# Hybrid attention layer on one core: pre-norm gain of token tiles 4 to 7 multiplied in by POOL, and a written-out order for all engines

## The chip, the core and the metric

One core of one Trainium2 chip. The core has a TensorE (PE), which multiplies matrices and transposes, a VectorE (DVE), a ScalarE (ACT), a GpSimd (POOL), and a SyncE (SP), whose queue here issues the DMA transfers. The metric is the time of one execution in microseconds (us) on the device, as the median of three runs.

## What is computed

One layer of an encoder for 1024 tokens of width 1024, all in float32. The reference, cut to what matters:

```python
h = rms_norm(x, norm_pre_g)                       # y * rsqrt(mean(y*y) + eps) * g
sb_q, sb_k, sb_v, sb_g, c_q, c_kv, k_rope, mla_g = split(h @ w_in)
sb_o  = stick_breaking_attention(sb_q, sb_k, sb_v)            # 8 heads of 64, strictly causal
sb_y  = head_rms_norm(sb_o, sb_out_norm_g) * silu(sb_g)
q     = rms_norm(c_q, q_norm_g) @ w_uq                        # 8 heads: 64 plain + 32 rotary
k_nope, v = split(rms_norm(c_kv, kv_norm_g) @ w_ukv)
mla_o = latent_attention(q_nope, rope(q_rope), k_nope, rope(k_rope), v)   # chunk-causal softmax
mla_y = head_rms_norm(mla_o, mla_out_norm_g) * silu(mla_g)
x = x + rms_norm(concat(sb_y, mla_y) @ w_out, norm_post_g)
x = x + rms_norm(p @ w_ple, ple_norm_g) * sigmoid(x @ w_ple_gate + b_ple_gate)
```

## The kernel before

**Precision and tiling.** Tokens go in eight tiles of 128. A float32 matrix product is made of three products of a faster type (float32r): each operand is split into a high half (a rounded copy) and a low half (the value less that copy), and high x high, high x low and low x high are added in PSUM. So most results go through the helper `split` (line 848): one copy, mostly on ACT, and one subtraction on DVE or POOL. The transposed, normalized input is kept as `hh` and `hl` (high and low halves, two buffers of four token tiles each). In the names of the trace, `h` is such a buffer, `u` and `f` are SBUF buffers of two pools (28 and 10 buffers of 4 KB per partition), `a` and `t` are PSUM banks of two pools (3 and 5), `ident` is the identity matrix for transposes.

**Stages.** First the value projection of the tiles (`xv_gen`, line 996, up to about 75 us), then the other projections, woven between 16 pairs of attention units (to about 625 us); `e1` (output projection and post-norm), `e2a` and `e2b` (gate product, made with seven instead of eight block products, and the final sum) end it. The per-layer embedding (`ple_gen`, line 1249) is one of the woven pieces; it transposes `p_in`, splits it into `pt`, and multiplies it by `w_ple`.

**The pre-norm (lines 889 to 931).** `x_norm(t)` squares a tile on ACT, makes the reciprocal root on POOL (`rstd_pow`, tile `sr`), and multiplies the tile by it on DVE. The gain `norm_pre_g` varies along the row, and can be put in at two places. With `t < GAINS` (line 69, 8: all tiles) it is put in behind the transposes, where it is one number per partition (`g_pre`): `x_tr(t)` makes, for each of eight blocks of 128x128, an ACT copy with that scale into `hh` and a DVE operation (`scalar_tensor_tensor`) into `hl`. Otherwise it is put in ahead of the transposes, along the row: by DVE in one step with `t < EARLY` (line 58), or else by POOL in a step of its own; `x_tr` then uses `split`, once for each half of the tile. `gain()` (line 905) spreads the gain over the partitions for these two cases; with `GAINS = 8` it isn't called.

**The order.** The body doesn't issue instructions; it records them (`Recorder.add`, line 414), 6,621 in all, 3,905 of them on PE. A list of numbers, `FLIP` (line 239), moves two-input operations between DVE and POOL, and copies between ACT and DVE. Each has a priority: its place in the recording, plus 336 in a piece marked low, plus a shift of its piece from the table `SHIFT` (line 76). `schedule` (line 533) then plays the program through with costs of its own: of the instructions of an engine that are ready, the one with the lowest priority number goes first. Buffers of a pool are handed out in the order of `turn`, also shifted by piece. `issue` (line 722) issues all in the order found; line 754 is the one line at which every instruction of the body stands in the trace. The engine queues run in that order, and the semaphores make each instruction wait for its inputs and its buffer.

**Other pieces the text speaks of.** `close` (in `e2b`, line 1669) makes an output piece: a DVE addition that reads PSUM, a sigmoid on ACT, a multiplication, an addition, and the store. The last block product of the program is made in two halves of 256 columns.

Of the kernel before, what the change touches and what calls it, by code (L numbers as in the profile page):

```python
# [1846 lines left out]
```

## Time and profile before

| | us |
|---|---|
| median of three runs | 765.4 |
| the three runs | 765.14, 765.4, 769.76 |
| the profiled execution, its own time | 765.5 |
| its span, from the first to the last instruction of the trace | 763.7 |

One execution is profiled; everything read from the trace belongs to it, and its time lies 0.1 us above the median. Its own time is 1.8 us more than its span. A busy time is the sum of what the trace gives for an engine's instructions. The ends of matmuls are modelled, so that successive ones overlap: two rows of PE can begin closer together than the first one lasts. Where the timeline puts a run of like instructions on one row, the row has the start of the first and the time to the end of the last.

### The profile page before, as it was taken

What the parts mean: (1) busy time and instruction counts of PE and PEld (TensorE: products, weight loads), DVE (VectorE), ACT (ScalarE), POOL (GpSimd) and SP (SyncE); (2) the same over time, 40 slices, a digit from 0 to 9 for tenths busy, and PEclk for the clock granted to TensorE, in tenths of its full rate; (3) what the DMA queues carried; (4) which work ended last, traced back from release to release, by engine and by line L of the source; (5) the groups of instructions that cost most, each with busy time, mean ns of one, the idle gap of its engine ahead of it and who ended that gap; (6) DMA issues with size and microseconds to landing.
All of it is one profiled execution on the core that took longest, in us unless ns stands there. A gap on an engine that the chain in (4) does not pass through costs nothing.

```text
span 763.7 us, 11831 instructions
## 1 busy us (share of the span) xinstructions
PE 751.0 (98%) x3905; PEld 621.0 (81%) x3905; DVE 630.6 (83%) x1238; ACT 399.7 (52%) x962; POOL 321.7 (42%) x306
## 2 busy tenths in 40 slices
PE   7999999999999999999999999999999999999997
PEld 4888998878888878888887788888888888888876
DVE  6966355599958869888888999989899998789987
ACT  7633133244534785666657767767765541451221
POOL 2141113104411269869888521430363126464642
PEclk9999999999999999999999999999999999999999
DMA  9753103587998643656545884878436367272332
GB/s 324 247 168 129 74 33 120 190 313 279 341 355 272 214 132 137 198 189 209 175 138 162 270 298 145 286 267 286 144 116 212 125 248 244 87 276 83 110 111 83
DMA packets 101982, 148.71 MB, mean 195 GB/s; under 512 B 7448, under 2 KB 55072, under 8 KB 101920
## 3 DMA queue, kind: packets, MB, share of 16 engines
q1 hardware_dynamic: 101920, 147.95, 57.3%
q8 instruction: 31, 0.51, 0.3%
q14 instruction: 31, 0.25, 0.1%
HBM read 101.26 MB, written 46.66 MB: 194 GB/s over the span
## 4 chain that ended last, share of the span: by engine, by line
PE 88%; ACT 5%; DVE 3%; DMA 2%; issue 1%; POOL 0%; SPq 0%; ACTq 0%; DVEq 0%; POOLq 0%
PE a L754 62%; PE t L754 26%; ACT u L754 3%; DVE u L754 1%; DMA u<-k_d 1%; DMA v_d<-f 1%; ACT L754 1%; ACT h L754 1%; ACT f L754 1%; DVE nm L754 1%; DVE f L754 1%; DMA u<-v_d 0%; SPq L754 0%; DVE t L754 0%; DVE nms L754 0%
## 5 line engine op out<-in xcount | busy, mean ns | idle before, releaser
L754 POOL TENSOR_TENSOR u<-u,u 128x512 f32<-128x512 f32 (+14 forms) x134 | 190.5, 1436 | 140.1 <-ACT u L754 74.8
L754 PE MATMUL a<-h,f 128*128 128x512 f32 x864 | 240.7, 404 | 0.0
L754 PEld LDWEIGHTS a<-h,f 128*128 128x128 f32 x864 | 155.2, 189 | 26.4
L754 DVE TENSOR_TENSOR u<-t,u 128x512 fp32r<-128x512 f32 (+4 forms) x284 | 150.6, 555 | 22.2 <-ACT u L754 12.8
L754 PE MATMUL t<-u,u 128*128 128x512 f32 (+4 forms) x580 | 151.0, 367 | 1.0 <-DMA u<-k_d 0.5
L754 PE MATMUL a<-u,u 128*128 128x512 f32 (+2 forms) x522 | 133.4, 370 | 0.1
L754 PE MATMUL t<-ident,u 128*128 128x128 f32 (+1 forms) x793 | 126.4, 273 | 1.4 <-DVE nms L754 0.5
L754 ACT CAST u<-t 128x512 fp32r<-128x512 f32 (+3 forms) x192 | 87.4, 490 | 75.4 <-PE t L754 49.0
L754 PEld LDWEIGHTS t<-u,u 128*128 128x128 f32 x580 | 103.0, 189 | 20.2 <-ACT u L754 3.2
L754 PE MATMUL a<-h,u 128*128 128x512 f32 (+1 forms) x492 | 117.3, 391 | 0.1
L754 ACT ACTIVATE u<-t 128x512 f32<-128x512 f32 (+5 forms) x208 | 92.0, 515 | 47.2 <-PE t L754 38.6
L754 PEld LDWEIGHTS t<-ident,u 128*128 128x128 f32 (+1 forms) x793 | 97.1, 140 | 22.3 <-DVE u L754 2.9
L754 PEld LDWEIGHTS a<-h,u 128*128 128x128 f32 x492 | 89.6, 188 | 20.3 <-DVE u L754 0.5
L754 PEld LDWEIGHTS a<-u,u 128*128 128x128 f32 x522 | 91.7, 188 | 16.9 <-DVE u L754 2.0
L754 DVE TENSOR_TENSOR u<-u,u 128x512 fp32r<-128x512 f32 (+8 forms) x88 | 79.6, 917 | 5.3 <-ACT u L754 3.5
L754 ACT ACTIVATE u<-t,nms 128x384 f32<-128x384 f32 (+5 forms) x96 | 55.2, 581 | 39.7 <-DVE nms L754 39.4
L754 DVE TENSOR_TENSOR_SCAN u<-u 128x320 f32<-128x320 f32 (+4 forms) x64 | 64.6, 1011 | 13.6 <-ACT u L754 12.4
L754 ACT ACTIVATE f<-a 128x512 bf16<-128x512 f32 (+2 forms) x64 | 34.2, 539 | 51.5 <-PE a L754 48.4
L754 POOL MEMSET u<- 128x128 f32 x64 | 13.0, 216 | 102.1 <-PE a L754 56.4
L754 DVE TENSOR_TENSOR u<-a,u 64x512 f32<-64x512 f32 (+4 forms) x75 | 47.8, 647 | 8.2 <-ACT u L754 6.9
L754 DVE TENSOR_REDUCE nm<-t 128x1 f32<-128x384 f32 (+5 forms) x96 | 51.8, 547 | 1.9 <-PE t L754 1.2
L754 PE MATMUL a<-u,h 128*128 128x512 f32 x192 | 47.0, 399 | 1.5 <-ACT h L754 1.4
(111 smaller groups left out, 801.1 us busy)
## 6 DMA issues: line engine op xcount, KB each, us to landing
u<-q_d SPq DMA_DIRECT2D x64, 256.0 KB, 4.4
u<-k_d SPq DMA_DIRECT2D x16, 512.0 KB, 5.1
u<-v_d SPq DMA_DIRECT2D x16, 512.0 KB, 5.4
u<-in_w_ple_gate_dram SPq DMA_DIRECT2D x16, 512.0 KB, 6.7
f<-in_w_in_dram SPq DMA_DIRECT2D x14, 512.0 KB, 5.1
v_d<-u SPq DMA_DIRECT2D x12, 512.0 KB, 3.1
f<-in_x_dram SPq DMA_DIRECT2D x9, 512.0 KB, 4.4
q_d<-u SPq DMA_DIRECT2D x9, 512.0 KB, 4.4
```

What stands on the lines that cost most here:

```text
L754: x["fn"](*[place(a) for a in x["args"]], **{k: place(a) for k, a in x["kw"].items()})
```

## The change

The gain of tiles 4 to 7 is put in ahead of the transposes, along the row, by POOL; tiles 0 to 3 stay as they were. `gain()` spreads the gain by one DMA. The order of every engine is now a table: `BASE` gives the priority of each of the 6,578 instructions, and `schedule` takes each engine's instructions strictly in that order instead of choosing among those that are ready; `TURNS` gives the turn of each tile for its buffer; `FLIP` is a new list, and `SHIFT` is empty. [...] The diff, with the tables cut to a line:

```diff
-EARLY = 7
+EARLY = 0
-GAINS = 8
+GAINS = 4
-SHIFT = {
-    0: (1204, 1209), 1: (-381, -413), 2: (-586, -394), 3: (-857, -953), 4: (-1159, -1106), 5: (-11, -91),
...
+SHIFT = {}
 FLIP = (
...
+BASE = (
+    17, 19, 15, 21, 16, 22, 18, 24, 2, 3, 4, 5, 6, 7, 8, 9, 10, 11, 12, 13, 31, 32, 35, 57, 26, 40, 39, 76, 53, 70,
...
+TURNS = (
+    28, 37, 33, 36, 2, 225, 298, 292, 287, 297, 306, 235, 308, 296, 304, 300, 317, 316, 310, 160, 283, 69, 58, 60,
...
@@ in Recorder.tile
-            self.tiles[key].update(turn=self.turn(1), turn0=len(self.ins), chunk=self.chunk)
+            self.tagged += 1
+            place = TURNS[self.tagged - 1] if TURNS else len(self.ins)
+            self.tiles[key].update(turn=place + SHIFT.get(self.chunk, (0, 0))[1], turn0=place, chunk=self.chunk)
@@ Recorder.turn
-    def turn(self, by=0):
-        return len(self.ins) + SHIFT.get(self.chunk, (0, 0))[by]
+    def turn(self):
+        i = len(self.ins)
+        return (BASE[i] if BASE else i + (LOW if self.low else 0) + self.bias) + SHIFT.get(self.chunk, (0, 0))[0]
@@ in schedule
+        line = {e: sorted((i for i in range(n) if ins[i]["eng"] == e), key=lambda i: (-ins[i]["prio"], -i))
+                for e in engines}
...
-                if avail[e]:
+                if BASE:
+                    if not line[e] or need[line[e][-1]]:
+                        continue
+                    s = max(free[e], ready[line[e][-1]])
+                elif avail[e]:
...
+            if BASE:
+                i = line[e].pop()
@@ gain
-                gb["pre"], row = k4(dt=F32, name="gb_pre"), k4(dt=F32, name="gb_row")
-            SP.dma_start(row[0:1], norm_pre_g[0:1, :])
-            for v in half:
-                ps = ps_t()
-                mm(ps, ones, row[0:1, v], start=True, stop=True)
-                ACT.copy(gb["pre"][:, v], ps)
+                gb["pre"] = k4(dt=F32, name="gb_pre")
+            bcast(gb["pre"], norm_pre_g, D)
```

The diff also adds four switches (`EVACS`, `NORMS`, `HALVES`, `SPREAD`) for other ways to make some steps. All are zero, and with zeros the steps are as before; `BYDVE` is now called `MASKER`.

What the new order looks like is shown at three places. The first is PE at the first tile of the per-layer embedding, whose `p_in` is `f_3760` before. Before:

```order
L754 MATMUL a_127<-u_3957,u_3534 128x384 x2
L754 MATMUL a_127<-u_3961,u_3534 128x256 x2
L754 MATMUL t_179<-ident,u_3796 128x128
L754 MATMUL t_179<-ident,u_3854 128x128
L754 MATMUL t_179<-ident,u_3937 128x128
L754 MATMUL a_127<-u_3767,u_3534 128x256 x2
L754 MATMUL t_172<-ident,f_3760 128x128
L754 MATMUL t_224<-ident,f_3760 128x128 x2
L754 MATMUL a_308<-f_3634,f_4051 128x512
L754 MATMUL a_308<-f_3658,f_4051 128x512
```

After; `f_3551` is now that `p_in`:

```order
L1074 MATMUL a_217<-u_3928,u_3710 128x384
L1074 MATMUL t_196<-ident,f_3551 128x128
L1074 MATMUL a_217<-u_3928,u_3710 128x384
L1074 MATMUL a_217<-u_3933,u_3710 128x256
L1074 MATMUL a_217<-u_823,u_3710 128x256
L1074 MATMUL a_217<-u_3760,u_3710 128x256
L1074 MATMUL a_217<-u_823,u_3710 128x256
L1074 MATMUL t_189<-ident,u_3763 128x128
L1074 MATMUL t_189<-ident,u_3826 128x128
L1074 MATMUL t_242<-ident,f_3551 128x128
L1074 MATMUL t_189<-ident,u_3904 128x128
L1074 MATMUL t_242<-ident,f_3551 128x128
```

Each tile of `p_in` needs two transposes into one bank (`t_172` before, `t_196` after; the first of the two stands further ahead), then its split copies, and then the matmuls that read them (`a_308` before, `a_251` after). Before, only two transposes of the next tile stand between the last transpose into `t_172` and the first matmul of `a_308`. After, five matmuls and five transposes stand between the last transpose into `t_196` and the first matmul of `a_251`, which is the row after these.

The second place is POOL at the start, where `sr` is the reciprocal root of a token tile's norm. Before:

```order
L754 TENSOR_TENSOR sr_168<-sm_166,nhalf 128x1
L754 TENSOR_TENSOR sr_199<-sm_194,nhalf 128x1
L754 TENSOR_TENSOR sr_270<-sm_266,nhalf 128x1
L754 TENSOR_TENSOR u_506<-f_361,u_506 128x512
L754 TENSOR_TENSOR sr_287<-sm_284,nhalf 128x1
L754 TENSOR_TENSOR u_533<-f_371,u_500 128x512
L754 TENSOR_TENSOR u_549<-f_365,u_549 128x128
L754 TENSOR_TENSOR f_568<-f_467,f_528 128x832
```

After; `u_321` is the gain, spread over all partitions, and `u_185`, `u_187` and `f_301` are token tiles:

```order
L1074 TENSOR_TENSOR sr_205<-sm_201,nhalf 128x1
L1074 TENSOR_TENSOR sr_280<-sm_274,nhalf 128x1
L1074 TENSOR_TENSOR u_185<-u_185,u_321 128x1024
L1074 TENSOR_TENSOR u_423<-u_255,u_403 128x1024
L1074 TENSOR_TENSOR u_187<-u_187,u_321 128x1024
L1074 TENSOR_TENSOR u_488<-u_327,u_447 128x1024
L1074 TENSOR_TENSOR u_485<-f_412,u_485 128x512
L1074 TENSOR_TENSOR sr_297<-sm_293,nhalf 128x1
L1074 TENSOR_TENSOR f_301<-f_301,u_321 128x1024
```

The multiplications by the gain stand between the last reciprocal roots and the low halves of the first weights. The DMA that spreads the gain is 16th in SP's queue.

The third place is the end, on DVE and on POOL, where the last output piece of 512 columns is closed. Before, on DVE:

```order
L754 TENSOR_TENSOR u_7213<-a_308,u_7213 128x512
L754 TENSOR_TENSOR u_6841<-a_235,u_6841 128x256
L754 TENSOR_TENSOR u_7135<-u_7135,u_7213 128x512
L754 TENSOR_TENSOR u_6841<-a_127,u_6841 128x256
L754 TENSOR_TENSOR u_6504<-u_6504,u_7135 128x512
L754 TENSOR_TENSOR u_6504<-u_6504,u_7135 128x256
L754 TENSOR_TENSOR u_7135<-u_7135,u_6841 128x256
L754 TENSOR_TENSOR u_6504<-u_6504,u_7135 128x256
```

and on POOL:

```order
L754 TENSOR_TENSOR u_7090<-u_7090,u_6826 128x512
L754 TENSOR_TENSOR u_7112<-u_7112,u_7213 128x512
L754 TENSOR_TENSOR u_7285<-u_7169,u_7285 128x512
L754 TENSOR_TENSOR u_6723<-u_6723,u_7112 128x512
L754 TENSOR_TENSOR u_7135<-u_7135,u_6841 128x256
```

After, on DVE:

```order
L1074 TENSOR_TENSOR u_6801<-a_143,u_6801 128x512
L1074 TENSOR_TENSOR u_7165<-u_7165,u_7141 128x512
L1074 TENSOR_TENSOR u_6801<-a_217,u_6801 128x256
L1074 TENSOR_TENSOR u_6735<-u_6735,u_7165 128x512
L1074 TENSOR_TENSOR u_6801<-a_251,u_6801 128x256
L1074 TENSOR_TENSOR u_7165<-u_7165,u_6801 128x256
```

and on POOL:

```order
L1074 TENSOR_TENSOR f_6505<-f_6505,u_7095 128x512
L1074 TENSOR_TENSOR u_7141<-u_7141,u_6699 128x512
L1074 TENSOR_TENSOR u_6902<-u_6902,u_7177 128x512
L1074 TENSOR_TENSOR u_7165<-u_7165,u_6801 128x256
L1074 TENSOR_TENSOR u_6735<-u_6735,u_7165 128x256 x2
```

The output tile is `u_6504` before and `u_6735` after. Before, DVE makes the last two additions of 256 columns; after, both are POOL's, and the last of them stands behind a multiplication that stays on DVE.

## Rows read from the trace of the kernel before

**Rows 1.** The page, its part 1: busy time, share of the span and number of instructions of each engine.

```profile
PE 751.0 (98%) x3905; PEld 621.0 (81%) x3905; DVE 630.6 (83%) x1238; ACT 399.7 (52%) x962; POOL 321.7 (42%) x306
```

**Rows 2.** Groups of PE's matmuls and transposes by shape, over the span: line, engine, operation, out<-in, shape, count | busy us, mean ns of one | idle time before them, and what ended it.

```profile
L754 PE MATMUL a<-h,f 128*128 128x512 f32 x864 | 240.7, 404 | 0.0
L754 PE MATMUL t<-ident,u 128*128 128x128 f32 x792 | 126.3, 273 | 1.4 <-DVE nms L754 0.5 <-DVE u L754 0.4 <-DVE sm L754 0.2
L754 PE MATMUL a<-h,u 128*128 128x512 f32 x468 | 114.5, 397 | 0.1
L754 PE MATMUL a<-u,u 128*128 128x512 f32 x334 | 97.9, 404 | 0.0
L754 PE MATMUL t<-u,u 128*128 128x512 f32 x235 | 67.4, 402 | 0.1
L754 PE MATMUL a<-u,h 128*128 128x512 f32 x192 | 47.0, 399 | 1.5 <-ACT h L754 1.4
L754 PE MATMUL a<-f,h 128*128 128x416 f32 x192 | 39.4, 357 | 0.7 <-DVE f L754 0.7
L754 PE MATMUL t<-u,u 128*128 128x384 f32 x115 | 30.2, 354 | 0.1
L754 PE MATMUL a<-f,f 128*128 128x512 f32 x96 | 29.0, 413 | 0.7 <-DVE f L754 0.3 <-ACT f L754 0.3
L754 PE MATMUL a<-u,u 128*128 128x256 f32 x125 | 24.1, 288 | 0.1
L754 PE MATMUL t<-u,u 128*128 128x448 f32 x80 | 23.2, 380 | 0.0
L754 PE MATMUL a<-u,u 128*128 128x384 f32 x63 | 18.7, 352 | 0.0
L754 PE MATMUL t<-u,u 128*128 128x320 f32 x80 | 17.1, 321 | 0.5 <-DMA u<-k_d 0.5
L754 PE MATMUL t<-u,u 128*128 128x256 f32 x70 | 16.6, 305 | 0.3 <-ACT u L754 0.3
L754 PE MATMUL t<-ident,f 128*128 128x128 f32 x80 | 12.0, 272 | 0.0
...
L754 PE MATMUL a<-still 128*128 128x512 bf16 x12 | 5.2, 627 | 2.2 <-DVE still L754 2.2
```

**Rows 3.** The timeline of PE, at 27, 403 to 408 and 640 us: start, us, engine, line, operation, out<-in, shape, count, and in brackets idle time before it and its releaser.

```profile
27.70 1.91 PE L754 MATMUL t<-ident,u 128*128 128x128 f32 x16
...
403.34 0.27 PE L754 MATMUL t<-ident,f 128*128 128x128 f32 x1
403.37 1.40 PE L754 MATMUL a<-u,u 128*128 128x512 f32 x5
404.61 0.60 PE L754 MATMUL t<-u,u 128*128 128x320 f32 x3
...
407.63 0.49 PE L754 MATMUL t<-ident,f 128*128 128x128 f32 x3
408.42 1.55 PE L754 MATMUL a<-f,f 128*128 128x512 f32 x5 [0.30 <-DVE f L754]
...
639.65 12.88 PE L754 MATMUL a<-h,u 128*128 128x512 f32 x55
```

**Rows 4.** The timeline of all engines at the end of the span, in the same columns.

```profile
750.04 8.56 PE L754 MATMUL a<-h,u 128*128 128x512 f32 x48
...
758.21 0.93 POOL L754 TENSOR_TENSOR u<-u,u 128x256 f32<-128x256 f32 x1 [0.87 <-ACT u L754]
...
758.98 1.84 DVE L754 TENSOR_TENSOR u<-u,u 128x512 f32<-128x512 f32 x4
```

**Rows 5.** The busy time of the engines by stretch: from:to, length, then busy us (and count) of PE, PEld, DVE, ACT and POOL, the granted clock of PE, the busy share of the DMA engines, and GB/s.

```profile
2.20:25.00 22.80, 21.00 (x87) 13.27 (x88) 16.23 (x43) 16.91 (x42) 4.99 (x8) 1.00 1.05 365
25.00:75.00 50.00, 50.00 (x240) 40.94 (x239) 36.91 (x95) 22.00 (x65) 11.52 (x11) 1.00 0.48 162
75.00:250.00 175.00, 174.31 (x883) 147.81 (x882) 121.34 (x275) 66.05 (x181) 38.10 (x52) 1.00 0.63 216
250.00:400.00 150.00, 149.89 (x834) 123.53 (x833) 126.36 (x200) 100.63 (x228) 114.98 (x101) 1.00 0.54 176
400.00:500.00 100.00, 97.52 (x544) 80.83 (x543) 93.18 (x220) 70.35 (x181) 44.15 (x41) 1.00 0.71 237
500.00:625.00 125.00, 124.70 (x707) 105.84 (x707) 115.70 (x241) 80.09 (x190) 33.98 (x37) 1.00 0.58 196
...
550.00:600.00 50.00, 50.00 (x277) 42.23 (x276) 47.09 (x92) 31.22 (x76) 20.20 (x22) 1.00 0.52 163
```

**Rows 6.** Groups by shape of ACT, DVE and POOL, in the columns of rows 2.

```profile
L754 DVE TENSOR_TENSOR u<-t,u 128x512 fp32r<-128x512 f32 x124 | 81.9, 680 | 14.0 <-ACT u L754 7.1 <-PE a L754 3.2 <-DMA k_d<-u 2.8
...
L754 ACT CAST u<-t 128x512 fp32r<-128x512 f32 x97 | 55.0, 599 | 42.7 <-PE t L754 27.2 <-PE a L754 7.5 <-DVE u L754 3.6
...
L754 DVE SCALAR_TENSOR_TENSOR h<-t,g_pre,h 128x128 fp32r<-128x128 f32 x64 | 17.6, 343 | 4.2 <-ACT h L754 4.0
...
L754 ACT ACTIVATE h<-t,g_pre 128x128 fp32r<-128x128 f32 x64 | 17.6, 396 | 2.8 <-PE t L754 1.9 <-DVE h L754 0.8
...
L754 POOL TENSOR_TENSOR f<-f,f 128x1024 fp32r<-128x1024 f32 x4 | 9.6, 2406 | 10.5 <-DVE f L754 10.5
```

**Rows 7.** The group of DVE's two-input operations of 128x512 with both inputs in SBUF, in the same columns.

```profile
L754 DVE TENSOR_TENSOR u<-u,u 128x512 fp32r<-128x512 f32 x32 | 30.1, 948 | 2.0 <-ACT u L754 1.9
```

More of the change, by code (lines that the diff above doesn't have):

```diff
@@ L359, in __init__ @@
         self.chunk = 0
+        self.tagged = 0
         self.thread = ""
@@ L655, in schedule @@
             s, e = best
[L656 to L659 removed]
+            if BASE:
+                i = line[e].pop()
+            else:
+                while pend[e] and pend[e][0][0] <= s:
+                    r, i = heapq.heappop(pend[e])
+                    heapq.heappush(avail[e], (ins[i]["prio"], i))
+                _, i = heapq.heappop(avail[e])
             x = ins[i]
@@ L838, in block_kernel @@
     gate_d = [dram([128, S], f"gate_d{i}") for i in range(8)]
+    rs_d = [dram([8, 128], f"rs_d{i}") for i in range(16)]
     y_d = dram([4, 128, KB, 2, 128], "y_d")
@@ L885, in x_load @@
         xt = k4(dt=F32, name="xt")
-        SP.dma_start(xt, x[0, t * 128:(t + 1) * 128, :])
+        for v in half if t == 0 and HALVES[0] else [slice(0, D)]:
+            SP.dma_start(xt[:, v], x[0, t * 128:(t + 1) * 128, v])
         x_tiles[t] = xt
@@ L891, in x_norm @@
         junk = k2((128, 1024), BF16, "junk")
-        ss, ms, rs = small("ss", 1, 4), small("sm", 1, 4), small("sr", 1, 4)
-        ACT.activation(junk, xt, AF.Square, accum_out=ss)
-        DVE.tensor_scalar(ms, ss, 1.0 / D, EPS, ALU.mult, ALU.add)
+        ss, ms, rs = small("ss", 2, 4), small("sm", 1, 4), small("sr", 1, 4)
+        if t == 0 and HALVES[0]:
+            for i, v in enumerate(half):
+                ACT.activation(junk[:, v], xt[:, v], AF.Square, scale=D ** -0.5, accum_out=ss[:, i:i + 1])
+            DVE.tensor_scalar(ms, ss[:, 0:1], ss[:, 1:2], EPS, ALU.add, ALU.add)
+        else:
+            ACT.activation(junk, xt, AF.Square, accum_out=ss[:, 0:1])
+            DVE.tensor_scalar(ms, ss[:, 0:1], 1.0 / D, EPS, ALU.mult, ALU.add)
         rstd_pow(rs, ms)
@@ L1027, in c_gen @@
         c_tr(NT - 1, last)
-    R.piece("warm") if hasattr(R, "piece") else None
     R.piece("warm")
@@ L1064, in proj, with qk_evac @@
         yield 1.3
-    def qk_evac(dst):
+    def qk_evac(dst, k):
         def evac(ps, n):
             t = k4((128, 2, 512), name="qkhl")
-            split(t[:, 0], t[:, 1], ps, heng=ACT)
+            if EVACS[2 * k + n]:
+                raw = k2(dt=F32, name="qkraw")
+                ACT.copy(t[:, 0], ps)
+                ACT.copy(raw, ps)
+                POOL.tensor_tensor(t[:, 1], raw, f(t[:, 0]), ALU.subtract)
+            else:
+                split(t[:, 0], t[:, 1], ps, heng=ACT)
             SP.dma_start(dst[:, :, half[n]], f(t))
@@ L1241, in half_norm @@
             ACT.activation(junk, ps, AF.Square, accum_out=ss[:, n:n + 1])
-            DVE.tensor_tensor(yg[:, half[n]], ps, gb[:, half[n]], ALU.mult)
+            if on_act:
+                ACT.copy(yg[:, half[n]], ps)
+            else:
+                DVE.tensor_tensor(yg[:, half[n]], ps, gb[:, half[n]], ALU.mult)
             yield 0.0
@@ L1272, in mms @@
                     yield 1.3
-                o, rs = yield from half_norm(mms, gb_ple, "ple_o")
-                DVE.tensor_scalar(o, o, rs, None, ALU.mult)
+                o, rs = yield from half_norm(mms, gb_ple, "ple_o", NORMS[t] == 1)
+                if NORMS[t] == 2:
+                    POOL.tensor_scalar(o, o, rs, None, ALU.mult)
+                elif NORMS[t]:
+                    DVE.scalar_tensor_tensor(o, o, rs, gb_ple, ALU.mult, ALU.mult)
+                else:
+                    DVE.tensor_scalar(o, o, rs, None, ALU.mult)
                 SP.dma_start(ple_d[t * 128:(t + 1) * 128, :], o)
@@ L1338, in sb_rows @@
                 ACT.activation(row[:, ks], ps[:, 0:h], AF.Sigmoid, scale=SB_SCALE)
+            if MASKER[4 * i[0] + 2 * i[1] + s] == 2:
+                for t, fill in ((u, 1.0), (row, 0.0)):
+                    t = t[:, nk - 128:nk]
+                    POOL.affine_select(t, t, pattern=[[-1, 128]], compare_op=ALU.is_gt, fill=fill, base=0,
+                                       channel_multiplier=1)
             ev, od = (slice(j, nk, 2) for j in range(2))
@@ L1451, in finish3 @@
         SP.dma_start(gl, gate_d[c][:, half[s]])
-        rx, ps = k2(dt=F32, name="rx"), ps_t()
-        ACT.copy(rx.rearrange("q (g d) -> q g d", d=64),
-                 bass.AP(tensor=rs.tensor, offset=rs.offset, ap=[rs.ap[0], [1, 8], [0, 64]]))
-        for a in range(4):
-            PE.transpose(ps[:, a * 128:(a + 1) * 128], rx[:, a * 128:(a + 1) * 128], ident)
-        DVE.tensor_tensor(ot, ps, ot, ALU.mult)
+        ps = ps_t()
+        if SPREAD[2 * c + s]:
+            PE.transpose(ps[0:8, 0:128], rs, ident)
+            rt, fac = k2((128, 128), F32, name="rt"), k2(dt=F32, name="fac")
+            ACT.copy(rt[0:8], ps[0:8, 0:128])
+            d = rs_d[2 * c + s]
+            SP.dma_start(d, rt[0:8])
+            for e in range(2):
+                SP.dma_start(fac[64 * e:64 * e + 64].rearrange("q (t n) -> q t n", t=4),
+                             d[4 * e:4 * e + 4].rearrange("(o t) n -> o t n", o=1).broadcast_to([64, 4, 128]))
+            choice(13).tensor_tensor(ot, ot, fac, ALU.mult)
+        else:
+            spread(ps, ot, rs)
         choice(14).tensor_tensor(ot, ot, gl, ALU.mult)
@@ L1464, in finish3, with spread @@
             SP.dma_start(y_d[:, :, c].rearrange("t q a n -> q t a n"), f(y))
+    def spread(ps, ot, rs):
+        rx = k2(dt=F32, name="rx")
+        ACT.copy(rx.rearrange("q (g d) -> q g d", d=64),
+                 bass.AP(tensor=rs.tensor, offset=rs.offset, ap=[rs.ap[0], [1, 8], [0, 64]]))
+        for a in range(4):
+            PE.transpose(ps[:, a * 128:(a + 1) * 128], rx[:, a * 128:(a + 1) * 128], ident)
+        DVE.tensor_tensor(ot, ps, ot, ALU.mult)
     def run_later(force=False):
@@ L1603, in e1 @@
         mms = big(ys, lambda kb, n: wo[0][n][:, kb], lambda kb, n: wo[1][n][:, kb])
-        yg, rs = yield from half_norm(mms, gb["post"], "yg")
+        yg, rs = yield from half_norm(mms, gb["post"], "yg", NORMS[8 + t])
+        if NORMS[8 + t]:
+            POOL.tensor_tensor(yg, yg, gb["post"], ALU.mult)
         DVE.scalar_tensor_tensor(xt, yg, rs, xt, ALU.mult, ALU.add)
@@ L1692, in e2b @@
                     R.piece(f"e{t}")
-                    close(1, 0, product(xs, 4, v), w, w, v, DVE)
+                    ps = product(xs, 4, v)
+                    step = 128 if v.start and HALVES[1] else 256
+                    for a in range(v.start, v.stop, step):
+                        close(1, 0, ps, w, w, slice(a, a + step), DVE)
                 continue
```

39 lines of the change are left out of this document (22 added, 17 removed), and 634 rows, old and new, of tables (BASE, FLIP, SHIFT, TURNS).

## The prediction

> **What bounds the kernel.** I read the page's totals first, then the PE stream in order of time, then its groups by shape, then the stretches, and only then single operations. The totals say that PE is busy 98% of the span [rows 1]. Busy time alone doesn't prove a PE limit, because the ends of matmuls are modelled: in the shape table a 512-column matmul "lasts" 404 ns [rows 2]. So I took the rate from a run without a wait: 55 of them fill 12.88 us, less the last one's 0.40, which is 0.231 us from start to start. Sixteen transposes fill 1.91 us, less the last one's 0.27: 0.109 us each [rows 3].
>
> With these the shape table [rows 2] gives the time that PE needs if nobody makes it wait. 2,189 matmuls of 512 columns x 0.231 = 505.9 us. The narrower ones by columns: 192 of 416 (36.1), 178 of 384 (30.8), 195 of 256 (22.5), 80 of 448 (16.2), 80 of 320 (11.6): 117.2. 872 transposes x 0.109 = 95.2. The twelve idle ones at the start: 5.2. That is 723.5 for 3,798 of 3,905; the other 107 cost 4 to 20 more. PE runs from 2.2 us (its idle time ahead of the first one, [rows 2]) to 758.6 (the last row of 48 starts at 750.04 and fills 8.56, [rows 4]): 756.4. So 12 to 29 us are lost to waits; I take 20. This is all that any order can win, since the change leaves the number and shapes of PE's 3,905 matmuls as they are.
>
> Where is it lost? The stretches [rows 5] show the granted clock at 1.00 throughout, and PE idle 1.8 us up to 25 us (22.8 less 21.0), nothing from 25 to 75, 0.7 up to 250, 0.1 up to 400, 2.5 from 400 to 500, 0.3 up to 625. Visible idle time is the smaller part, and I share the rest out like it: 2.5 of these 5.4 is nearly half of 20, but that stretch also has the longest single waits, which show most; I take 7 us for 400 to 500. DVE is busy 93.2 of 100 us there.
>
> The time sum is made against the profiled execution: 765.5 us, 1.8 more than its span, and 0.1 above the median of the three runs. A measurement of this kernel can tell about 1%, 7.7 us, from no change.
>
> **Part 1: the gain of tiles 4 to 7.** Removed: 32 ACT and 32 DVE operations of 128x128, each 17.6/64 = 0.275 us [rows 6], 8.8 us on either engine. Added: 8 copies of 128x512 (five on ACT at 0.60, three on DVE at 0.68) and 8 subtractions on DVE at 0.68. ACT is relieved by 5.8 us and DVE by 1.4. POOL gets four multiplications of 128x1024; the nearest row is 2.41 us, so 9.6 us. None of this lies on the path of the end: from 25 to 75 us, where these tiles are made ready, PE is busy 50.00 of 50 while POOL works 11.5 and ACT 22.0 [rows 5]. What hides the multiplications is POOL's idle time; if that cover is gone, each is a link ahead of eight transposes, and what then is late is PE (a rival below). Queued behind a multiplication on POOL are the next rstd power and the low halves of weights. Value 0; bounds: -0.5 (an earlier evacuation) and +9.6. The row of the gain, now spread over all partitions, is one more DMA of 0.52 MB in SP's queue, 16th there, behind the x tiles. In the first 25 us the DMAs move 365 GB/s [rows 5], so later transfers can slip by 1.4 us: 0, up to +1.4.
>
> **Part 2: finer interleaving on PE.** In PE's order I count 254 runs of transposes before and 455 after. The price of a cut is read at a lone transpose: from 403.34 to 404.61 stand one transpose and five matmuls [rows 3]; 1.27 less 5 x 0.231 is 0.115, against 0.109 within a run. 201 more runs x 0.006 = +1.2 us; bounds 0 and twice that.
>
> **Part 3: who does what.** Matching the two orders, 62 two-input operations go from DVE to POOL and 69 from POOL to DVE; 91 copies go from DVE to ACT and 74 back. By the time at which they stand in the trace, and with the durations of like shapes, DVE loses 9.0 us of work from 75 to 250, gains 16.7 from 250 to 400 (26 operations come from POOL, 5 go), loses 4.5 from 400 to 500 and 8.2 from 500 to 625. In 400 to 500, where DVE is short, I count its relief in full, 4.5 us, and add 0.46 for one wait that the order itself removes: three transposes at 407.63 need 0.33, and the matmul that reads their copy starts at 408.42, released by DVE [rows 3]. After the change five matmuls stand between the first of these transposes and its matmul. Together -5.0; bounds 0 and -7. Elsewhere, 75 to 250 and 500 to 625, 1.0 us of PE is visibly idle: -0.5, bounds 0 and -1.5. For 250 to 400 I take 0: DVE rises from 126.4 to some 143 of 150 us, 95%, but from 550 to 600 it is at 94% and PE waits for nothing [rows 5]. The bound is +7.5, worked out as a rival.
>
> [...] DVE's subtraction with one input in PSUM takes 0.68 us; with both inputs in SBUF it takes 0.95 on average for the same shape [rows 6, 7]. [...]
>
> **Part 4: the end.** The last multiply-add after PE's last matmul moves in part to POOL: the final addition of 256 columns now runs there. Its nearest row is 0.93 us; DVE's last four take 1.84 together, 0.46 each [rows 4]. So +0.5; bounds 0 and +1.0 (the first half's two operations are now POOL's as well).
>
> **Sum.** 0 + 1.2 - 5.0 - 0.5 + 0 + 0.5 = -3.8: 765.5 - 3.8 = **761.7 us**, half a per cent faster. Its own range is 758 to 766.
>
> **Rivals.** *Most waits go.* The order is made anew for every instruction, and the 13 us that I leave lost outside 400 to 500 are within its reach. All 7 there and half of the 13 gone, plus 1.7 for parts 2 and 4: 765.5 - 13.5 + 1.7 = 753.7. For it: PE's need doesn't grow, and the crowded engine of each stretch is relieved (POOL in 250 to 400, DVE in 400 to 625). Against it: waits are spread thin, a few tenths each.
>
> *DVE becomes the bound from 250 to 400.* Its 26 new operations make it 95% busy over 150 us. From the point where DVE falls behind PE's order, PE loses as it does now from 400 to 500, 7 in 100: 10.5, of which I put 3 down as lost already. With no relief in 400 to 500 either, as its own order is as tight, 765.5 + 7.5 + 1.7 = 774.7, slower. Against it: 550 to 600, and that POOL has fewer operations there to hold DVE up.
>
> [...]
>
> *POOL's gain is late.* PE stands before the transposes of four tiles for 2.4 us each: 761.7 + 9.6 = 771.3. It decides if POOL's multiplication ends after PE reaches that tile. Against it: POOL is idle more than three quarters of that stretch.
>
> **How the numbers follow.** Forecast 0.40 (761.7); most waits go 0.34 (753.7); DVE from 250 to 400 0.13 (774.7); port 0.08 (767.2); late gain 0.05 (771.3). More than 1% faster, below 757.8, is the second alone: 0.34. More than 1% slower, above 773.2, is the third alone: 0.13. Within 1%: 0.40 + 0.08 + 0.05 = 0.53. The range for 8 in 10 reaches from 752, a little below the best case, to 771, which leaves out most of the worst.
>
> **What would show it.** Right: PE starts and ends its 3,905 matmuls with the same two rates; its idle time from 400 to 500 falls from 2.5 us to under 1; DVE's busy time there falls by some 4 us; PE has none from 25 to 75; the span's end lies 5.3 to 6 us behind PE's last matmul instead of 5.1. Wrong in size: PE idle in 250 to 400 above 2 us (then DVE there), or PE's last matmul before 750 (then the waits outside 400 to 500 went too). Wrong in mechanism: idle PE ahead of transposes between 25 and 75 us with POOL as releaser, or transposes that cost more than 0.12 us alone.

## The result, and the profile after

The changed kernel takes 758.5 us (median of four runs, 757.3 to 760.13), 8.1 us less than the kernel before in the same comparison (766.6); the ratio is 0.9891, with an interval of 0.9876 to 0.9906. That is 1.1% faster, at the edge of what can be told, and inside the range given for the forecast (758 to 766), at its lower end. The forecast gain was 3.8 us, so the measured one is more than twice that. The profiled execution took 757.3 us, the fastest of the four; its span is 755.2.

The totals of the page, which answer to [rows 1]:

```profile
PE 744.9 (99%) x3905; PEld 617.3 (82%) x3905; DVE 602.4 (80%) x1207; ACT 399.5 (53%) x948; POOL 319.3 (42%) x303
```

PE has the same 3,905 instructions, and DVE is busy 28 us less. The stretches after, in the columns of [rows 5]:

```profile
2.00:25.00 23.00, 21.79 (x96) 14.87 (x97) 16.84 (x44) 16.88 (x43) 6.10 (x10) 1.00 1.02 357
25.00:75.00 50.00, 50.00 (x241) 41.20 (x240) 28.72 (x65) 19.87 (x46) 20.93 (x15) 1.00 0.51 178
75.00:250.00 175.00, 175.00 (x894) 149.03 (x893) 115.69 (x274) 66.79 (x192) 50.68 (x56) 1.00 0.63 216
250.00:400.00 150.00, 148.68 (x826) 121.57 (x825) 133.23 (x228) 96.77 (x212) 84.72 (x81) 1.00 0.54 175
400.00:500.00 100.00, 100.00 (x576) 84.45 (x575) 94.44 (x226) 74.95 (x191) 46.85 (x46) 1.00 0.77 253
500.00:625.00 125.00, 125.00 (x698) 104.95 (x697) 109.71 (x228) 81.94 (x193) 44.84 (x42) 1.00 0.58 191
```

PE is idle in 250 to 400 us now (1.3), and no longer in 400 to 500 and 75 to 250. But the stretches are of time, and PE is ahead of before by 2 us at 25 and by 8 at 500; so from here on I go by PE's own progress: matmuls and transposes are numbered in PE's order, 0 to 3,904. **Loss** is the time from the start of each matmul to the next, less what its shape takes at full rate, which I read from runs of like ones without a wait in the trace of before (0.2315 us for 512 columns, down to 0.118 for 256; 0.1095 for a transpose), summed over the records; the 0.08 us by which a matmul behind a transpose starts early in the records (one starts 0.03 us behind the transpose at 403.34, [rows 3]) are put back.

```
matmul no.   about, us (before)   loss before   loss after
   0-88           2-25                3.5           1.7
  88-326         25-75                0.3           0.1
 326-1207        75-250               3.1           1.3
1207-2030       250-398               3.8           4.8
2030-2590       398-501               6.8           1.8
2590-3286       501-625               2.0           1.2
3286-3905       625-758               0.7           0.2
all                                  20.2          11.1
```

One line of the table holds luck. In the traces of this order at that place (the kernel after and eight kernels below), a wait of 0.7 to 0.9 us at matmul 2624 stands in six of nine; the profiled execution of the kernel after is one of the three without it. So its 1.2 us for 2590 to 3286 would more often be some 2 us, as in the kernel before, and the win there isn't shown. It goes with which of two operations starts first, a DVE addition of 8 columns, `ms<-ms,e`, or POOL's next one, which a DMA releases. In the kernel after, DVE comes first:

```profile
497.99 0.16 DVE L1074 TENSOR_TENSOR ms<-ms,e 128x8 f32<-128x8 f32 x1
```

```profile
498.52 1.29 POOL L1074 TENSOR_TENSOR u<-u,u 128x512 f32<-128x512 f32 x1 [0.98 <-DMA u<-gate_d]
```

In two_on_dve (below), whose order is the same there, POOL comes first by 0.2 us, and DVE's addition ends at 498.35 us, POOL's operation at 498.33:

```profile
497.24 1.11 DVE L1185 TENSOR_TENSOR ms<-ms,e 128x8 f32<-128x8 f32 x1
```

```profile
497.05 1.28 POOL L1185 TENSOR_TENSOR u<-u,u 128x512 f32<-128x512 f32 x1 [0.25 <-DMA u<-gate_d]
```

In all six traces with the wait POOL starts 0.12 to 0.32 us ahead of DVE, whose addition takes 0.99 to 1.19 us; in the three without it POOL starts 0.12 to 0.53 us behind, and the addition takes 0.16.

9.1 us less loss, and 0.7 us more behind the last matmul, make the 8.5 us by which the span is shorter (PE also begins 0.1 us earlier). All visible waits of PE after, by releaser (us in total, times, longest):

```profile
PE a L1074 <- DVE still L1074: 2.1, 1, 2.1
PE a L1074 <- ACT h L1074: 1.1, 1, 1.1
PE a L1074 <- DVE u L1074: 0.7, 2, 0.5
PE t L1074 <- DVE u L1074: 0.6, 2, 0.3
```

The wait for the copies of `p_in`, 0.30 us ahead of `a<-f,f` in [rows 3], is gone. PE's timeline there now:

```profile
403.77 0.27 PE L1074 MATMUL t<-ident,f 128*128 128x128 f32 x1
403.80 0.90 PE L1074 MATMUL a<-u,u 128*128 128x384 f32 x5
...
405.00 1.18 PE L1074 MATMUL a<-f,f 128*128 128x512 f32 x4
```

The second transpose of the tile at 403.77, its matmul at 405.00, and no wait between: five matmuls and other transposes fill the time that DVE needs for its two operations (a copy at 404.08 and a subtraction that ends at 404.96).

### The profile page after: what moved, and what is told of

It reads as the page before. It is cut to its first block, busy times and chain, and to the rows that moved or that the text cites. A ratio compares the mean times of both kernels' runs of the same rounds, so it can differ in the third digit from the quotient of the medians.

```text
span 755.2 us, 11746 instructions
## 1 busy us (share of the span) xinstructions
PE 744.9 (99%) x3905; PEld 617.3 (82%) x3905; DVE 602.4 (80%) x1207; ACT 399.5 (53%) x948; POOL 319.3 (42%) x303
## 4 chain that ended last, share of the span: by engine, by line
PE 94%; issue 2%; DVE 2%; POOL 1%; ACT 1%; DMA 1%; POOLq 0%; DVEq 0%
PE a L1074 66%; PE t L1074 28%; DVE u L1074 2%; POOL u L1074 1%; ACT u L1074 1%; DMA gate_d<-f 1%; POOL f L1074 0%; DVE f L1074 0%; POOLq L2210 0%; ACT f L1074 0%; POOL ident masks.py:199 0%; DVE eye L1074 0%; DVE still L1074 0%; ACT g_pre L1074 0%; DVE sm L1074 0%
## 5 line engine op out<-in xcount | busy, mean ns | idle before, releaser
L1074 PE MATMUL a<-h,f 128*128 128x512 f32 x864 | 271.0, 413 | 0.0
L1074 POOL TENSOR_TENSOR u<-u,u 128x512 f32<-128x512 f32 (+15 forms) x139 | 192.0, 1394 | 168.8 <-ACT u L1074 73.2
L1074 PE MATMUL t<-u,u 128*128 128x512 f32 (+4 forms) x584 | 170.5, 367 | 0.3 <-DVE u L1074 0.3
L1074 PE MATMUL t<-ident,u 128*128 128x128 f32 (+1 forms) x793 | 154.0, 272 | 0.3 <-DVE u L1074 0.3
L1074 PE MATMUL a<-u,u 128*128 128x512 f32 (+2 forms) x521 | 152.2, 377 | 0.5 <-DVE u L1074 0.5
L1074 PE MATMUL a<-h,u 128*128 128x512 f32 (+1 forms) x492 | 129.4, 396 | 0.0
L1074 DVE TENSOR_TENSOR u<-u,u 128x512 f32<-128x512 f32 (+12 forms) x100 | 78.8, 800 | 10.6 <-ACT u L1074 5.9
L1074 DVE TENSOR_TENSOR_SCAN u<-u 128x320 f32<-128x320 f32 (+5 forms) x64 | 59.2, 929 | 7.3 <-ACT u L1074 6.7
L1074 ACT ACTIVATE f<-a 128x512 bf16<-128x512 f32 (+3 forms) x64 | 34.5, 542 | 48.2 <-PE a L1074 38.1
L1074 PEld LDWEIGHTS a<-u,h 128*128 128x128 f32 x192 | 34.8, 188 | 9.6 <-ACT h L1074 1.3
```

Source lines behind the costliest of these rows:

```text
L1074: x["fn"](*[place(a) for a in x["args"]], **{k: place(a) for k, a in x["kw"].items()})
```

## The experiments

Twelve kernels ran beside the kernel before. Those made from the kernel after carry its order as ranks and its buffer of every tile as a table, which gives the same order on every engine; so an instruction can be moved or given to another engine with all else at its place. Sums of loss are by the table above.

**The gain alone, under the old rule** (gain_alone). In the kernel before:

```diff
-GAINS = 8
+GAINS = 4
-EARLY = 7
+EARLY = 0
-            SP.dma_start(row[0:1], norm_pre_g[0:1, :])      # and a product on PE, two copies
+            bcast(gb["pre"], norm_pre_g, D)
```

> The kernel before with the gain of tiles 4 to 7 moved to POOL and spread by one DMA, and nothing else: the old rule for the order, with its shifts by piece, and the old choice of engines. If the written order brings the 8 us (my theory), this is within 3 us of before: 763 to 769 (ratio 0.996 to 1.004), with PE's loss from 400 to 500 us still near 6.9 us. If the gain's relief of ACT and DVE brings them, 757 to 761 (ratio under 0.994). PE should have no idle time behind POOL from 25 to 75 us under either.

804.7 us, ratio 1.050 (1.047 to 1.052): both ranges were missed; only the last sentence held, as no wait of PE there has POOL as its releaser. Loss is 63.7 us, spread over the program, and some 10 us of the rise are the clock: its mean is 0.986 over the span, against 0.999 before (an estimate: the difference of 0.013, of 807 us). The likely reason is that the shifts of the old table belong to one list of instructions, of which 64 are gone and 21 added: by the names and shapes of its tiles PE's order differs from before at 1,858 of 3,905 places, up to matmul 3444. That this is the whole reason isn't shown, since the gain's place changed as well.

**The moves alone, under the old rule** (moves_old_rule). As above, and:

```diff
 FLIP = (
-    (the list of before, renumbered)
+    (the list of after)
```

> As the run with the gain alone, and also with the new choice of engines (136 changes between DVE and POOL, 168 between ACT and DVE), but still ordered by the old rule with its old shifts. If the moves bring the gain, 757 to 761, with PE's loss from 400 to 500 us at 3 us or less. If the order does, there is no gain: 764 to 775, since the old shifts were not made for these engines.

810.3 us, ratio 1.056 (1.054 to 1.058), loss 61.1, of it 14.0 for matmuls 2030 to 2590. So it gives no gain without its order; but it can't be told from the run before, in which the old order is lost already. These two say nothing of the parts, only that neither gains under the old table.

**The order with the old engines** (order_old_engines). In the kernel after:

```diff
 FLIP = (
-    (the list of after)
+    (the list of before, renumbered)
```

> The kernel after, with each instruction at its place in the written order and in its buffer, but the old choice of engines: what DVE, POOL and ACT exchanged goes back, and stands in its engine's line where the written order has it. If the order brings the gain by putting other work between a result and the matmul that needs it, most of it stays: 757 to 761 (ratio under 0.994), loss from 400 to 500 us at 2 to 3.5 us. If the moves do, it is gone: 762 to 768 (ratio over 0.995), loss there at 5 us or more. Above 770 the two are only good together.

793.4 us, ratio 1.035 (1.032 to 1.037). Loss is 47.4, and 7.4 for matmuls 2030 to 2590, about as much as before has (6.8). This is the third of the expected cases: the order isn't good with the old engines either.

**The gain undone in the new order** (order_old_gain). In the kernel after, the 64 operations at the places of the 16:

```diff
-GAINS = 4
+GAINS = 8
```

> The kernel after with only the gain undone: for tiles 4 to 7 it goes back behind the transposes, as 32 ACT and 32 DVE operations of 128x128 in the places of the 16 that they replace; order, buffers and engines are otherwise those of after. If the gain is worth nothing by itself, 757 to 760, as after. If it is worth what it takes off ACT and DVE, slower than after by 2 us or more, with the loss between 25 and 75 us.

762.8 us, ratio 0.994 (0.992 to 0.996), 4.3 more than after. Between 25 and 75 us the loss rises from 0.1 to 2.9, behind DVE's `h` and `f`: there this order counts on the engines being relieved (before, whose order was made for the gain behind the transposes, loses 0.3 there). Another 3.3 us are lost between matmuls 2130 and 2200, far from the edit; the profiled execution was the slowest of six (760.4 to 764.1), so not each of them need have this. There the two traces differ in which of two operations is the long one. DVE and POOL in the kernel after:

```profile
413.29 0.68 DVE L1074 TENSOR_TENSOR u<-u,u 128x512 fp32r<-128x512 f32 x1
```

```profile
413.27 2.10 POOL L1074 TENSOR_TENSOR u<-u,u 128x766 f32<-128x766 f32 x1
```

The same instructions with the gain undone:

```profile
416.05 2.06 DVE L1183 TENSOR_TENSOR u<-u,u 128x512 fp32r<-128x512 f32 x1
```

```profile
416.02 1.54 POOL L1183 TENSOR_TENSOR u<-u,u 128x766 f32<-128x766 f32 x1
```

DVE's operation with two inputs in SBUF takes 0.68 us in the one and 2.06 in the other; POOL's takes 2.10 and 1.54. They start all but together: in seven traces (the kernel after, head_old_pe, head_old_act, gain_twice, two_on_dve, close_on_dve, combined) DVE starts 0.009 to 0.020 us behind POOL and takes 0.68; in this one and in mid_old_engines it starts 0.029 and 0.023 behind and takes 2.06 and 2.07. So the longest lag with 0.68 and the shortest with some 2.06 are 0.003 us apart; whether the edit or chance made the lag longer is open. PE then waits 0.56 and 1.07 us by its timeline, and pays again, in the granted clock (behind the busy time and count of PE):

```profile
421.00:422.00 1.00, 0.30 (x3) 0.97 0.50 78
422.00:425.00 3.00, 3.00 (x11) 0.50 0.96 319
```

From 422 to 425 us, right behind the waits, the granted clock is 0.50. In mid_old_engines (below) the same two waits, 0.58 and 1.07 us at the same matmuls, aren't followed by this:

```profile
419.37 0.66 PE L1184 MATMUL t<-ident,u 128*128 128x128 f32 x4 [1.07 <-DVE u L1184]
```

```profile
422.00:425.00 3.00, 3.00 (x19) 1.00 0.83 265
```

**The middle: PE's order of before** (mid_old_pe). In the kernel after, 240 of PE's ranks are handed out anew:

```diff
 BASE = (
-    (ranks of matmuls 2030-2130, 2200-2400 in the order of after)
+    (the same ranks, in the order of before)
```

> The kernel after, with PE's matmuls 2030 to 2130 and 2200 to 2400 (about 395 to 413 and 426 to 460 us) in the order of before; engines, other lines and buffers as after. There before loses 3.6 us and after 0.9. If the order on PE is what took the waits away, 2 to 3.5 us of loss come back there, with waits ahead of matmuls a<-f,f and of transposes: 759.5 to 762. If the relief of DVE by the moved operations did, the loss there stays at 0.9 to 1.7 and the time under 759.

767.0 us, ratio 0.9999 (0.999 to 1.001): the whole gain is gone. Loss in the two pieces is 9.2, not 2 to 3.5, since PE now stands for results that the other engines' lines bring in another order:

```profile
PE t L1185 <- ACT u L1185: 4.8, 6, 1.5
```

**The middle: the old engines** (mid_old_engines). In the kernel after:

```diff
 FLIP = (
-    (after, for 27 operations between 395 and 493 us)
+    (before, for these)
```

> The kernel after, with the old engines for the 27 operations that changed hands and run between 395 and 493 us (12 copies of ACT and 4 operations of POOL go to DVE, 7 copies of DVE to ACT, 4 operations of DVE to POOL); all orders as after. If the moves are needed, the loss from matmul 2030 to 2590 rises from 1.8 to 4.5 to 7 us (6.8 in before): 761 to 764. If the order alone carries it, it stays under 3 us: 757 to 759.5.

763.9 us, ratio 0.996 (0.994 to 0.997). Loss of matmuls 2030 to 2590 is 8.3, more than expected:

```profile
PE t L1184 <- DVE u L1184: 2.8, 5, 1.1
...
PE a L1184 <- DVE u L1184: 1.8, 4, 0.6
```

Each of the two edits gives back about the 5.0 us that were won in the stretch, or more: 9.3 and 6.6, of which 1.7 in mid_old_engines are the meeting at matmuls 2144 to 2150 shown above. Both leave lines of engines together that weren't made for each other, so what they lose isn't the worth of the part taken out. These runs give order and moves no shares of the gain. A new order made for the old engines, which would, was not run.

**The start: PE's order of before** (head_old_pe).

```diff
 BASE = (
-    (ranks of PE's first 60, in the order of after)
+    (the same ranks, in the order of before)
```

> The kernel after, with PE's first 60 matmuls and transposes in the order of before, all else as after. If the 1.8 us that PE gains up to 25 us come from the matmuls that the new order puts between tile 1's transposes and the matmul that reads their copies, that wait comes back: one wait of about 1.0 us released by ACT's h near 11 to 13 us, 758.5 to 760 in all. If they come from earlier loads or an earlier evacuation, the loss up to 25 us stays under 2.3 us and the time within 0.5 us of after.

759.2 us, ratio 0.990 (0.988 to 0.991); loss up to matmul 88 is 2.0, not 2.6 or more, and kernels with an unchanged start show 1.6 to 2.1. My theory fell: the wait doesn't come back. It is ACT's order. Before, ACT squares token tile 2 (`u<-u`, 1.09 us) ahead of the first scaled copies of tile 1, and PE has to wait for them:

```profile
11.31 1.09 ACT L754 ACTIVATE u<-u 128x1024 bf16<-128x1024 f32 x1
...
12.35 0.92 ACT L754 ACTIVATE h<-t,g_pre 128x128 fp32r<-128x128 f32 x3
...
12.80 4.76 PE L754 MATMUL a<-u,h 128*128 128x512 f32 x19 [0.90 <-ACT h L754]
```

After, the copies come first:

```profile
11.78 1.40 ACT L1074 ACTIVATE h<-t,g_pre 128x128 fp32r<-128x128 f32 x5 [0.15 <-PE t L1074]
...
11.93 4.46 PE L1074 MATMUL a<-u,h 128*128 128x512 f32 x18
...
13.04 1.08 ACT L1074 ACTIVATE u<-u 128x1024 bf16<-128x1024 f32 x1
```

**The start: ACT's order of before** (head_old_act). One rank in `BASE`, of the square of tile 2:

```diff
-    93,
+    78.5,
```

> The kernel after, with one ACT instruction moved: the square of token tile 2 (1.2 us) stands ahead of tile 1's scaled copies, as in before, and not behind five of them. After head_old_pe, my theory is that this place on ACT, and not PE's order, took the wait of 1.1 us near 12 us away: PE then waits 0.8 to 1.5 us for ACT's h near 12 to 13 us, and the loss up to 25 us goes from 1.7 to between 2.6 and 3.5 us; 758.5 to 760. If the early gain comes from the loads, the loss there stays under 2.2 us. A wait of the square for its tile's load would make it more.

759.8 us, ratio 0.991 (0.989 to 0.993); loss up to matmul 88 is 3.1, as was expected, of 3.5 before. The copies start at 12.80, behind the square, and PE waits:

```profile
11.76 1.11 ACT L1185 ACTIVATE u<-u 128x1024 bf16<-128x1024 f32 x1
...
12.80 0.68 ACT L1185 ACTIVATE h<-t,g_pre 128x128 fp32r<-128x128 f32 x2
...
13.28 3.04 PE L1185 MATMUL a<-u,h 128*128 128x512 f32 x12 [0.47 <-ACT h L1185]
```

**The cover of the gain** (gain_twice). Each multiplication made twice:

```diff
             POOL.tensor_tensor(xt, xt, gain(), ALU.mult)
+            POOL.tensor_tensor(xt, xt, gain(), ALU.mult)
```

> The kernel after, with each of POOL's four multiplications by the gain made twice (so tiles 4 to 7 carry the gain squared). If POOL's idle time hides the gain, as the prediction says, 9.6 us more of POOL's work cost little: loss between 25 and 75 us under 1 us, 757 to 759.5. If each multiplication is a link ahead of a tile's transposes with no room left, PE stands for up to 2.4 us a tile: 2 to 9.6 us there, 760 to 768.

768.6 us, ratio 1.002 (1.000 to 1.004): loss of matmuls 88 to 326 goes from 0.1 to 9.3, near the whole 9.6 us. PE's waits there:

```profile
29.83 1.09 PE L1186 MATMUL t<-ident,u 128*128 128x128 f32 x8 [1.46 <-POOL u L1186]
...
39.34 0.50 PE L1186 MATMUL a<-h,u 128*128 128x512 f32 x1 [2.18 <-POOL u L1186]
...
49.91 0.33 PE L1186 MATMUL t<-ident,f 128*128 128x128 f32 x1 [1.13 <-POOL f L1186]
...
62.03 0.33 PE L1186 MATMUL t<-ident,u 128*128 128x128 f32 x1 [2.01 <-POOL u L1186]
```

POOL's line there has the multiplications of two tiles and two of 128x1024 for weights in one piece, and behind it the weight's low half that PE waited for at 39.34:

```profile
24.94 14.35 POOL L1186 TENSOR_TENSOR u<-u,u 128x1024 f32<-128x1024 f32 x6
39.25 1.29 POOL L1186 TENSOR_TENSOR u<-f,u 128x512 fp32r<-128x512 f32 x1
```

So the gain is hidden, but with next to no room: POOL is idle 58% of that stretch in the kernel after (20.93 busy of 50), and not in the places where it would count.

**POOL beside DVE's scans** (two_on_dve). In the kernel after, two of POOL's multiplications go to DVE, which is the busier one over 250 to 400 us (133.2 us against 84.7):

```diff
 FLIP = (
+    2718, 2752,
```

In the kernel after, DVE's scans of 64 and 128 columns near 316 and 318 us:

```profile
316.21 1.70 DVE L1074 TENSOR_TENSOR_SCAN u<-u 128x64 f32<-128x64 f32 x1
...
318.02 2.13 DVE L1074 TENSOR_TENSOR_SCAN u<-u 128x128 f32<-128x128 f32 x1
```

and POOL beside them:

```profile
313.57 4.19 POOL L1074 TENSOR_TENSOR u<-u,u 128x512 f32<-128x512 f32 x2
...
317.87 2.58 POOL L1074 TENSOR_TENSOR u<-u,u 128x1022 f32<-128x1022 f32 x2
```

> The kernel after, with two multiplications of POOL near 315 and 318 us (894 and 1022 columns, both inputs in SBUF) made by DVE at the same place of the order. In the trace of after two DVE scans of 64 and 128 columns took 1.70 and 2.13 us there beside POOL's operations, against 0.26 and 0.40 at best, and PE waited 0.4 and 0.5 us behind them. [...]

Two cases were expected. If POOL's operations beside them make the scans long, they take 0.26 to 0.6 us here, PE's loss from 250 to 395 us falls from 4.8 to 3.9, and the whole takes 756.5 to 759; if DVE's load is what counts, that loss is 5.5 or more, and the whole takes 759 to 761.

DVE with the two operations (894 and 1022 columns) added:

```profile
316.14 0.29 DVE L1185 TENSOR_TENSOR_SCAN u<-u 128x64 f32<-128x64 f32 x1
316.35 1.07 DVE L1185 TENSOR_TENSOR u<-u,u 128x894 f32<-128x894 f32 x1
...
317.54 0.41 DVE L1185 TENSOR_TENSOR_SCAN u<-u 128x128 f32<-128x128 f32 x1
317.87 1.49 DVE L1185 TENSOR_TENSOR u<-u,u 128x1022 f32<-128x1022 f32 x1
```

The scans take 0.29 and 0.41 us, in place of 1.70 and 2.13: the first case. The stretch from 310 to 322 us in the kernel after, in the columns of [rows 5]:

```profile
310.00:322.00 12.00, 11.43 (x65) 8.84 (x64) 10.75 (x14) 4.40 (x12) 10.74 (x10) 1.00 0.63 193
```

and with the two on DVE:

```profile
310.00:322.00 12.00, 11.97 (x69) 9.36 (x69) 10.50 (x17) 5.03 (x13) 7.60 (x8) 1.00 0.62 185
```

DVE does 2.5 us more and is busy 0.25 us less (of the same stretch of time, in which PE is 0.6 us further on). The loss of matmuls 1207 to 2030 falls from 4.8 to 4.1, and the two visible waits are gone. In the time of the whole, 757.8 us (ratio 0.988, 0.986 to 0.990), this can't be told from the kernel after.

**The end on DVE** (close_on_dve). The last closing in two halves without POOL:

```diff
 FLIP = (
-    6558, 6559, 6576,
```

The end of the kernel after, POOL and DVE:

```profile
749.73 1.53 POOL L1074 TENSOR_TENSOR u<-u,u 128x256 f32<-128x256 f32 x2 [1.49 <-ACT u L1074]
...
750.62 0.92 DVE L1074 TENSOR_TENSOR u<-u,u 128x256 f32<-128x256 f32 x1 [0.48 <-ACT u L1074]
751.62 0.72 POOL L1074 TENSOR_TENSOR u<-u,u 128x256 f32<-128x256 f32 x1 [0.36 <-DVE u L1074]
```

> The kernel after, with the last closing in two halves of 256 columns (two multiplications, two additions) all on DVE. By the rows of after, POOL's 0.72 us addition at the end becomes one of DVE at 0.42 to 0.46, and DVE's last multiplication, which took 0.92 beside POOL's two operations, takes 0.42: the end comes 0.6 to 0.9 us earlier, 5.2 to 5.5 us behind PE's last matmul's start plus its length instead of 6.0. [...] In the time of the whole this is near what can be told: 756.5 to 758.3.

The end with DVE alone:

```profile
749.52 1.01 DVE L1184 TENSOR_TENSOR u<-u,u 128x512 f32<-128x512 f32 x2
...
750.46 0.41 DVE L1184 TENSOR_TENSOR u<-a,u 128x256 f32<-128x256 f32 x1
...
751.35 0.88 DVE L1184 TENSOR_TENSOR u<-u,u 128x256 f32<-128x256 f32 x2 [0.15 <-ACT u L1184]
```

From the start of PE's last matmul to the end of the last compute instruction it is 2.7 us, 3.2 in the kernel after and 2.5 before: 0.5 won, a little less than expected, likely since DVE's addition that reads the second half (750.46) now stands behind the first half's final addition. To the end of the span only 0.3 is won (6.05 to 5.78). 757.8 us, ratio 0.988 (0.986 to 0.989): too little to tell from after in the time.

**Together** (combined).

```diff
 FLIP = (
+    2718, 2752, 3089, 3218,
-    6558, 6559, 6576,
 BASE = (   # the first half's last addition, behind the second half's first
-    (rank of 6559)
+    (rank of 6573) + 0.5
```

> The kernel after, with four multiplications of POOL made by DVE (the two of two_on_dve, and two of 448 and 384 columns near 348 and 366 us, each beside a DVE scan of the same unit that took 2.30 and 1.99 us there against 1.06 and 0.94 at best), and with the last closing on DVE, whose addition of the second half's PSUM now stands ahead of the first half's final addition. [...] If DVE has no room for the two operations near 348 and 366 us, the waits at 350 and 371 us (0.4 and 0.7 us) stay or grow: 757 to 759.

756.1 us, ratio 0.987 (0.985 to 0.989). That lies in the 755.5 to 757.5 expected if POOL's operations make the scans long, with a loss of 3.2 to 3.8 from 250 to 395 us. Loss of matmuls 1207 to 2030 is 2.9, the waits at 350 and 371 us are gone, and the end is at 2.75 us, as in close_on_dve and not earlier: the first half's multiplication still stands ahead of the addition that reads the second half. It is the fastest median of all; its interval still overlaps that of after, so against after it is shown by its trace (10.0 us of loss in place of 11.1, though it has the wait at matmul 2624 and the other has not), not by its time.

A graft of all lines of before into one stretch of after was not tried: the buffers' turns don't allow it.

## Why the prediction was right, and where it was not

*The whole.* The forecast was right within its range and low by half: -3.8 us against -8.1. That the time lies inside 758 to 766 is in part luck, since the kernel before took 766.6 us in this comparison and not 765.4; as a gain, 8.1 us is just more than the 7.5 at the end of that range. PE's last matmul starts at 749.1 us, which the prediction had named as the sign that waits outside 400 to 500 us went too.

*The base.* 20 us of loss, 7 of them from 400 to 500: measured 20.2 and 6.8. The reading of the rate from runs without a wait held.

*Part 1, the gain: 0.* It cost nothing in this order. The upper bound, 9.6, was the right price (9.2 with twice the work). But the reason, POOL's idle time, was weak: it doesn't lie where the chain runs. And undoing the relief of ACT and DVE, which I took for nothing, costs 2.8 us there in this order; against before, whose order does without it, the stretch won 0.2.

*Part 2, the cuts: +1.2.* About half of it. The steps beside transposes that lose under 0.04 us each sum to 1.2 us before and 1.7 after, at the rates of the loss table; a rate wrong by 1 ns would move either sum by over 1 us.

*Part 3, 400 to 500: -5.0.* Measured -5.0 (6.8 to 1.8). The size was right; its make-up, 4.5 for the moves and 0.46 for the order, is not borne out: undoing PE's order or the moves in this stretch costs 9.3 or 6.6 us, and no run gives the parts by themselves. That forecast and measurement agree to a tenth is then luck. Nor did DVE's busy time in that stretch of time fall by 4 us: it rose from 93.18 to 94.44, with 32 more matmuls in the stretch; for the same matmuls, by number, it fell from 93.2 to 89.6.

*Part 3, elsewhere: -0.5.* This is the step that failed. For 75 to 250 us 1.8 us were won (3.1 to 1.3; 0.84 of it is one wait at 82 us, the rest is in pieces of under 0.2), and up to 25 us, where I counted nothing, 1.8. For 501 to 625 the traces show 0.8, which is the wait at matmul 2624 and mostly isn't won. I had let visible idle time stand for what can be won (1.0 us), though the base held 20 us of loss and only 5.4 of visible idle time. For the start I had no term at all, only 1.8 us of idle time in a row; an order on ACT was behind most of it, as head_old_act shows (1.4 of the 1.8 come back).

*Part 3, 250 to 400: 0.* Measured +1.0, and for another reason than DVE's sum of work. I had DVE rise by 16.7 us; for the same matmuls it rose by 7.4 (126.3 to 133.7), with 32 us less of POOL's busy time beside it. An estimate from the two traces fits: take the shortest tenth of the durations of each shape as what it needs, and the rest as stretch. By it DVE's need rose by 17.7 us there, as I had it, while its stretch fell from 26.5 to 19.2; over the whole kernel it fell from 70 to 52. That POOL causes this stretch is shown for the scans of two_on_dve (1.70 to 0.29 us, 2.13 to 0.41), not for all. Of the 4.8 us lost there 1.9 went when four of POOL's operations were taken away; the rest was not traced.

*Part 4, the end: +0.5.* Measured +0.7 (5.38 to 6.05 us from the start of PE's last matmul to the end of the span); 0.3 to 0.5 of it is the closing on POOL and what it does to DVE's multiplication, as close_on_dve shows (0.92 us for it beside POOL's two operations; there, without them, 0.88 for a multiplication and an addition together).

*The rivals.* The result lies between the forecast (761.7) and "most waits go" (753.7), somewhat nearer the first: outside 400 to 500 us 4.1 us of loss went, where I had 0.5 and that rival 6.5. By the ratio it is just past the 1% that I had given to the second alone, by the time (758.5) it is not below its 757.8. The chance called port (0.08, 767.2) is for POOL's new operations holding DVE up as long as they relieve it; no run shows a port, only how long the operations took. The relief was not given back: by the estimate above, DVE's stretch for matmuls 2038 to 3285 is 11.7 us before and 12.0 after. That POOL holds DVE up is borne out: DVE's operations of [rows 7], with both inputs in SBUF, took 0.95 us before and 0.78 after, with half as many of them (16), and where POOL's operation was taken away the scan fell from 1.70 to 0.29. At matmul 2624, where the starts lie 0.12 us or more apart, the order of the starts goes with the time of DVE's addition (0.16 us ahead of POOL, 0.99 to 1.19 behind it); at 413 us, where DVE starts 0.009 to 0.029 us behind POOL, its operation takes 0.68 or 2.06. What I missed is the sign: the 64 scans, of the same sizes, take 64.6 us before and 59.2 after.

## What to carry to other kernels

Where one engine is at 98%, sum the loss against its full rate by its own progress, not by time and not from visible idle time alone: that sum bounds what an order can win (here 9.1 of 20.2), and no stretch of it is out of reach for having no visible idle time. Don't share out a plan's gain to its order and its moves; undo one locally, with all else pinned, and read which wait comes back. Look at the same place in several traces of one order before you count a win of under 1 us there. Before giving work to POOL, look whether it will run beside a DVE operation that the busy engine waits for: here a scan took 1.70 us beside POOL's operations and 0.29 without them, and an addition of 8 columns 1.11 in place of 0.16.
